# A hybrid encoder layer on one core: the low half of every second weight block made by a negated copy and an accumulating transfer

## The chip, the cores and the metric

The kernel runs on one core of a Trainium2 chip. The core has five engines that run side by side, each with its own queue of instructions: TensorE (PE: matmuls; PEld: its weight loads), VectorE (DVE), ScalarE (ACT), GpSimd (POOL) and SyncE (SP). Sixteen DMA engines move data between DRAM and the on-chip memory; a transfer is issued from the queue of an engine. The metric is the device time of one execution in microseconds (us), the median of several runs.

## The reference, cut to what matters

One layer of an encoder with 512 tokens of width 2048. Everything is float32.

```python
h = rms_norm(x, norm_w)                       # (512, 2048)
proj = h @ w_in                               # w_in (2048, 4608): q, k, v, attention gate, lru input, lru gate
q, k, v, g_attn, xr, g_lru = split(proj)
attn = attention(rope(norm(q)), rope(norm(k)), v)          # 8 heads of 128, 2 kv heads
lru = scan_forward(conv(xr)) + scan_backward(conv(xr))     # gated linear recurrence, 1024 wide
mixed = concat(rms_norm(attn) * silu(g_attn), rms_norm(lru) * silu(g_lru))
out = x + mixed @ w_out                       # w_out (2048, 2048)
```

## The kernel before

**Split products.** TensorE multiplies in a float32 format that keeps fewer bits (fp32r in the profile). To keep accuracy, every operand is held as a high half, its value rounded to that format, and a low half, the remainder. A product takes three matmuls: high by high, high by low, low by high (`mm3`, lines 143 to 145). So each weight has to be split before TensorE can use it.

**Weight blocks.** The input projection goes over blocks of 256 rows by 512 columns of `w_in`, eight blocks for each group of 512 columns. `wraw` loads a block of 512 KB with one transfer on SyncE's queue (line 191) into one of three raw buffers `wr`, laid out as two slabs of 128 partitions by 512. `wsplit` turns one slab into its halves: ScalarE casts the slab to `wh` (line 202), and VectorE subtracts the cast from the slab into `wl` (line 203). `wload` does that for both slabs, k = 0 and k = 1. Each pool has four buffers of `wh` and four of `wl`, which is two blocks. A second pool, `wx`, is opened inside the key and value step of the Q stage and closed when the Q stage is done; while it is open, `turn_of` makes the two slabs of a block alternate between the pools, so four blocks fit.

A block is used by 24 matmuls: four output tiles, for each of them both slabs, for each slab the three products. `proj_feat` (lines 276 to 300) has the weights stationary, `tok_block` (lines 302 to 312) has them moving. A buffer is free when the last of the four output tiles has used it.

**Order of the stages.** Projection of the recurrence's input (16 blocks), of keys and values (8), of Q (16), of the gates (three times 8), of the last gate (8), and then the output projection with `w_out`, which has its own loads and splits (lines 665 to 702) and does not call `wload`. The first projections are interleaved with the recurrence (`lru_half`), Q with the key and value preparation (`kv`), and the three gates with `attention`, which yields after each step so that two pieces of projection are placed between (`STEPS`, line 43). In attention, VectorE takes the row maximum (line 561), ScalarE the exponential (line 564), GpSimd scales the weights (line 566), and TensorE transposes them two steps later (line 573).

**Who sets the order.** The order of TensorE's instructions is as written. On the other engines a planner in the framework orders the instructions by priority and by its own estimate of when they can start; loads and splits of weights get a higher priority by `AHEAD` (line 37), so they are placed as early as their buffers permit. Each engine then runs its queue strictly in that order. GpSimd issues no transfer in this kernel: its queue holds small reciprocal square roots (lines 254 and 255), the scaling of line 566, and sums of squares (line 595). The kernel is built with 1024 bytes of each partition set aside for the descriptors of such transfers (line 1003).

Of the kernel before, what the change touches and what calls it, by code (L numbers as in the profile page):

```python
# [12 lines left out]
AF = mybir.ActivationFunctionType  # L13
ALU = mybir.AluOpType
AX = mybir.AxisListType

P = 128
SEQ = 512
# [37 lines left out]
def hybrid_kernel(  # L56
# [20 lines left out]
    nc = tc.nc  # L77
# [6 lines left out]
    def opened(name, side):  # L84
        pools[name] = tc.alloc_tile_pool(name=name, bufs=1, side=side, reuse_waits="tile")
        order[side].append(name)
        return pools[name]

    def closed(*names):
        for name in names:  # L90
            for side in order.values():
                if side and side[-1] == name:
                    side.pop()
                    pools.pop(name).release()
# [11 lines left out]
    def nm(s):  # L106
        cnt[0] += 1
        return f"{s}_{cnt[0]}"
# [30 lines left out]
    def f(ap):  # L139
        return ap.bitcast(F32)  # L140
# [44 lines left out]
    def wraw(w, r0, c0, nk=1, queue=nc.sync):  # L185

        raw = pools["wr"].tile([P, 2, SEQ], F32, tag="wr", bufs=3, name=nm("wr"))
        src = w[r0 : r0 + 2 * P, c0 : c0 + SEQ].rearrange("(k p) e -> p k e", p=P)
        for k in range(nk):
            ks = slice(k * 2 // nk, (k + 1) * 2 // nk)  # L190
            queue.dma_start(raw[:, ks, :], src[:, ks, :])
            yield raw

    turn_of = [0]

    def wsplit(raw, k):

        turn_of[0] += k
        pool = pools["wx" if "wx" in pools and turn_of[0] % 2 else "xw"]
        hi = pool.tile([P, SEQ], F32R, tag="wh", bufs=4, name=nm("wh"))  # L200
        lo = pool.tile([P, SEQ], F32R, tag="wl", bufs=4, name=nm("wl"))
        nc.scalar.copy(hi, raw[:, k, :])  # L202
        nc.vector.tensor_sub(lo, raw[:, k, :], f(hi))  # L203
        return hi, lo

    def wload(w, r0, c0):
        with tc.high_priority(AHEAD):
            (raw,) = wraw(w, r0, c0)
            return [wsplit(raw, k) for k in range(2)]


    xh, xl = [None] * KT, [None] * KT
# [63 lines left out]
    def proj_feat(c0, acc, first=None, given={}):  # L276

        acc += [pj() for _ in range(4)]
        for c in range(KT // 2):
            if c == 0 and first:  # L280

                for k, (wh, wl) in enumerate(first):
                    for j, (w, x_) in enumerate(((wh, xh), (wl, xh), (wh, xl))):
                        for e in range(4):
                            nc.tensor.matmul(  # L285
                                acc[e], w[:, e * P : (e + 1) * P], x_[k],
                                start=k == 0 and j == 0, stop=False,
                            )
                            if (j, e) in ((1, 1), (2, 3)):
                                yield c, 2 * k + j - 1  # L290
                        if (k, j) == (0, 0):
                            yield None
                continue
            ws = given[c] if c in given else wload(w_in, c * 2 * P, c0)
            for e in range(4):
                es = slice(e * P, (e + 1) * P)
                for k, (wh, wl) in enumerate(ws):
                    kk = 2 * c + k
                    mm3(acc[e], wh[:, es], wl[:, es], xh[kk], xl[kk], kk == 0, kk == KT - 1)
                yield c, e  # L300

    def tok_block(acc, w, r0, c0, lh, ll, nk):

        acc += [pj() for _ in range(NT)]
        for c in range(nk // 2):
            ws = wload(w, r0 + c * 2 * P, c0)
            for t in range(NT):
                ts_ = slice(t * P, (t + 1) * P)
                for k, (wh, wl) in enumerate(ws):
                    kk = 2 * c + k  # L310
                    mm3(acc[t], lh[kk][:, ts_], ll[kk][:, ts_], wh, wl, kk == 0, kk == nk - 1)
                yield c, t
# [4 lines left out]
    def weave(fill, chain):  # L317

        for n in chain:
            for _ in range(n):  # L320
                next(fill, None)
# [46 lines left out]
    def lru_half(half, acc):  # L368

        grs = []  # L370
        for n in range(4 * half, 4 * half + 4):
            gr = k2(shape=(P, 4, P))
            with tc.high_priority(AHEAD):
                nc.sync.dma_start(gr[:, 0:2, :], lru_wa[:, n].rearrange("d c e -> c d e"))
                nc.sync.dma_start(gr[:, 2:4, :], lru_wx[:, n].rearrange("d c e -> c d e"))
            grs.append(gr)
        xrs = evac_bc(acc)
        for b in range(0, 4, 2):
            bs = slice(b, b + 2)
            steps = ((6, 4, 8, 4), (10, 5, 8, 5))[half][bs]  # L380
            yield from lru_pair(4 * half + b, xrs[bs], grs[bs], steps, 99 if half and b else 0)
# [436 lines left out]
    with tc.high_priority():  # L818
        xs, ws = xload(0, 2), wraw(w_in, 0, C_XR, 2, nc.scalar)
        xc, raw = next(xs), next(ws)  # L820
        nc.scalar.dma_start(nw_st, norm_w.rearrange("(k p) -> k p", p=P))
        next(xs), next(ws)
        table = const([P, 1], "table")
        nc.scalar.activation(table, ones[:, :1], AF.Exp)
        columns(nw, nw_st)
        first = [wsplit(raw, 0)]
        xturn(xc, 0)
        busy(WARM2)
    chunks = [xchunk(c) for c in range(1, KT // 2)]
    loads, turns = iter(chunks), iter(chunks)  # L830
    for step in proj_feat(C_XR, a1, first, given):
        if step is None:
            with tc.high_priority():
                first.append(wsplit(raw, 1))
                xturn(xc, 1)
            xsquare(xc, 0)
            next(next(loads), None)
            given[1] = wload(w_in, 2 * P, C_XR)
            continue
        c, e = step  # L840
        if (e == 0 or e == 2) and c:
            next(next(loads, iter(())), None)
        if (e, c) == (2, 0) or (e == 1 and c) or (e, c) in ((3, 1), (3, 2)):
            next(next(turns, iter(())), None)
        if (c, e) == (1, 2):
            given[2] = wload(w_in, 4 * P, C_XR)
            s2.close()
        if (c, e) == (2, 3):
            vec_load()
        if (c, e) == (5, 3):  # L850
            columns(vec, vec_st)
        if (c, e) == (KT // 2 - 1, 0):
            with tc.high_priority():
                xstats()
# [9 lines left out]
    def kv_proj():  # L864
        yield from proj_tok(C_K, a3)
        kvs.extend(
            evac_tok(
                a3, lambda: pools["rope"].tile([P, SEQ], F32, tag="kv", bufs=NT, name=nm("kv"))
            )
        )  # L870

    weave(kv_proj(), lru_half(1, a2))
    closed("lru")
    opened("rot", "left")
    opened("qkv", "right")
    rots = []
# [141 lines left out]
```

## Time and profile before

| | |
|---|---|
| median of 2 runs | 669.88 us (669.74 to 670.03) |
| span of the profiled execution | 668.2 us, 9513 instructions |
| the runs' times beyond that span | 1.5 to 1.8 us (the profiled execution's own time is told by its span) |
| TensorE | 662.1 us, 99% |
| VectorE | 486.2 us, 73% |
| ScalarE | 331.5 us, 50% |
| GpSimd | 56.8 us, 8% |
| transfers | 71.06 MB, mean 106 GB/s |

The span goes from the first to the last instruction. A row of a group of instructions reads: line, engine, operation, written tile <- read tiles, shapes, count; then busy time and the mean ns of one; then the idle time of the engine ahead of them and what ended it. A row of the timeline begins with the start in us and the duration. TensorE's matmuls are pipelined: a row's duration is longer than the distance between the starts of two of them.

### The profile page before, as it was taken

The numbers are of one execution on the slowest core, as the hardware profiler recorded it, in microseconds if no ns is written. First come the engines' busy times: TensorE is split into PE (matmuls) and PEld (weight loads), VectorE is DVE, ScalarE is ACT, GpSimd is POOL, SyncE is SP. The second block draws the span as 40 slices with busy tenths as digits, with TensorE's granted clock in tenths as the row PEclk, the third lists the DMA queues.
The fourth block names the chain that finished last, engine by engine and source line by source line (L and its number), as shares of the span: only waits on it lengthen the run. The fifth ranks groups of instructions, "written<-read, shape, count | busy, mean of one in ns | idle before, by whom it ended". The sixth has DMA issues, their size and how long they took to land.

```text
span 668.2 us, 9513 instructions
## 1 busy us (share of the span) xinstructions
PE 662.1 (99%) x3607; PEld 570.9 (85%) x3607; DVE 486.2 (73%) x819; ACT 331.5 (50%) x581; POOL 56.8 (8%) x77
## 2 busy tenths in 40 slices
PE   8999999999999999999999999999999999999997
PEld 6888888888888888888888888888889999899996
DVE  4879688977687853756955668439979994976944
ACT  3543799489766416445643455335436333332320
POOL 0000000000021302121222112110000000000000
PEclk9999999999999999999999999999999999999999
DMA  8843252322244311421122211232335364362711
GB/s 286 273 138 95 64 157 71 96 63 70 89 126 127 98 60 36 122 64 54 41 65 64 63 40 56 63 95 66 94 124 187 99 214 129 116 211 88 244 40 63
DMA packets 43773, 71.06 MB, mean 106 GB/s; under 512 B 2776, under 2 KB 13136, under 8 KB 43728
## 3 DMA queue, kind: packets, MB, share of 16 engines
q1 hardware_dynamic: 43408, 69.93, 34.2%
q8 instruction: 28, 0.46, 0.3%
q10 hardware_dynamic: 320, 0.53, 0.3%
q14 instruction: 17, 0.14, 0.1%
HBM read 66.25 MB, written 4.19 MB: 105 GB/s over the span
## 4 chain that ended last, share of the span: by engine, by line
PE 99%; DMA 1%; ACTq 0%; DVE 0%; issue 0%
PE pj L143 19%; PE pj L145 19%; PE pj L144 19%; PE pj L727 10%; PE mm L727 8%; PE mm L748 6%; PE mm L145 3%; PE mm L144 3%; PE mm L143 3%; PE mm L573 2%; PE mm L228 1%; PE pj L285 1%; PE mm L521 1%; DMA nw_st<-in_norm_w_dram 1%; PE mm L265 0%; PE mm L641 0%
## 5 line engine op out<-in xcount | busy, mean ns | idle before, releaser
L143 PE MATMUL pj<-x,wh 128*128 128x512 f32 x376 | 149.8, 398 | 0.0
L145 PE MATMUL pj<-x,wl 128*128 128x512 f32 x376 | 146.7, 390 | 0.0
L144 PE MATMUL pj<-x,wh 128*128 128x512 f32 x376 | 146.5, 390 | 0.0
L202 ACT CAST wh<-wr 128x512 fp32r<-128x512 f32 x144 | 86.6, 618 | 75.8 <-PE pj L145 28.8
L203 DVE TENSOR_TENSOR wl<-wr,wh 128x512 fp32r<-128x512 f32 x144 | 100.2, 716 | 30.7 <-ACT wh L202 30.5
L145 PEld LDWEIGHTS pj<-x,wl 128*128 128x128 f32 x376 | 70.6, 188 | 15.2
L144 PEld LDWEIGHTS pj<-x,wh 128*128 128x128 f32 x376 | 70.8, 188 | 13.8 <-issue 0.5
L143 PEld LDWEIGHTS pj<-x,wh 128*128 128x128 f32 x376 | 70.6, 188 | 13.6 <-issue 0.5
L143 PE MATMUL pj<-wh,x 128*128 128x512 f32 x192 | 75.9, 395 | 0.0
L144 PE MATMUL pj<-wl,x 128*128 128x512 f32 x192 | 75.1, 391 | 0.0
L145 PE MATMUL pj<-wh,x 128*128 128x512 f32 x192 | 75.0, 391 | 0.0
L727 PE MATMUL pj<-wh,ml 128*128 128x256 f32 x192 | 54.1, 282 | 0.0
L727 PE MATMUL pj<-wh,mh 128*128 128x256 f32 x192 | 54.0, 281 | 0.0
L727 PE MATMUL pj<-wl,mh 128*128 128x256 f32 x192 | 53.8, 280 | 0.0
L684 ACT CAST wh<-wr 128x768 fp32r<-128x768 f32 x24 | 20.1, 837 | 62.2 <-issue 46.6
L575 ACT CAST b<-mm 128x512 fp32r<-128x512 f32 x32 | 18.8, 586 | 59.8 <-PE mm L573 59.8
L561 DVE TENSOR_REDUCE mx<-mm 128x1 f32<-128x512 f32 x32 | 22.0, 689 | 31.1 <-PE mm L145 30.6
L145 PEld LDWEIGHTS pj<-wh,x 128*128 128x128 f32 x192 | 36.1, 188 | 8.1
L143 PEld LDWEIGHTS pj<-wh,x 128*128 128x128 f32 x192 | 36.0, 188 | 8.0 <-issue 0.2
L144 PEld LDWEIGHTS pj<-wl,x 128*128 128x128 f32 x192 | 36.1, 188 | 7.9 <-issue 0.2
L727 PE MATMUL mm<-wh,ml 128*128 128x256 f32 x144 | 40.5, 282 | 0.0
L727 PE MATMUL mm<-wh,mh 128*128 128x256 f32 x144 | 40.5, 281 | 0.0
(207 smaller groups left out, 1334.0 us busy)
## 6 DMA issues: line engine op xcount, KB each, us to landing
wr<-in_w_in_dram SPq DMA_DIRECT2D x71, 512.0 KB, 3.6
wr<-in_w_out_dram SPq DMA_DIRECT2D x32, 512.0 KB, 4.0
xt<-in_x_dram SPq DMA_DIRECT2D x16, 256.0 KB, 4.4
out_dram<-xt SPq DMA_DIRECT2D x15, 256.0 KB, 3.6
b<-in_x_dram SPq DMA_DIRECT2D x7, 512.0 KB, 7.6
k<-in_lru_wa_dram SPq DMA_DIRECT2D x8, 128.0 KB, 3.8
k<-in_lru_wx_dram SPq DMA_DIRECT2D x8, 128.0 KB, 3.2
wr<-in_w_in_dram ACTq DMA_DIRECT2D x2, 256.0 KB, 4.7
```

Of the source, the lines that this page charges most:

```text
L143: nc.tensor.matmul(acc, lh, rh, start=start, stop=False)
L144: nc.tensor.matmul(acc, lh, rl, start=False, stop=False)
L145: nc.tensor.matmul(acc, ll, rh, start=False, stop=stop)
L202: nc.scalar.copy(hi, raw[:, k, :])
L203: nc.vector.tensor_sub(lo, raw[:, k, :], f(hi))
L228: nc.tensor.transpose(pt[:, t * P : (t + 1) * P], xc[:, t, ks], ident)
L561: nc.vector.tensor_reduce(mx, sc, axis=AX.X, op=ALU.max, negate=True)
L573: nc.tensor.transpose(pt[:, s * P : (s + 1) * P], p[:, s * P : (s + 1) * P], ident)
L575: nc.scalar.copy(pth[:, :, tt], p3)
L684: nc.scalar.copy(hi[:, to], part)
L727: nc.tensor.matmul(dst, lh[:, a, ts_], rh[:, b_, :], start=bank in fresh, stop=last and s == 1 and rh is bh and lh is al, skip_group_check ...
L748: nc.tensor.matmul(dst, lh[:, a, ts_], rh[:, w], start=new, stop=last and k == 1 and j == 2, skip_group_check=True,)
```

## The change

`wsplit` gets a third argument, the place of the slab in DRAM. Without it nothing is different. With it, the low half is made in two steps: ScalarE writes minus the high half into `wl`, and then GpSimd issues a transfer that reads the slab a second time from DRAM and adds it onto `wl`. `wload` passes the place for the second slab (k = 1) of each block, once the flag `summing` is set; the flag is set after the key and value projection, ahead of Q. So it applies to 48 blocks: Q, the three gates, and the last gate. The raw slab itself is still loaded, since the high half is cast from it. The other changed lines set and read the flag.

```diff
-    def wsplit(raw, k):
+    summing = [False]
+
+    def wsplit(raw, k, src=None):
...
         nc.scalar.copy(hi, raw[:, k, :])
-        nc.vector.tensor_sub(lo, raw[:, k, :], f(hi))
+        if src is None:
+            nc.vector.tensor_sub(lo, raw[:, k, :], f(hi))
+        else:
+            nc.scalar.activation(lo, f(hi), AF.Copy, scale=-1.0)
+            nc.gpsimd.dma_start(lo, src, accum_op=ALU.add)
         return hi, lo
 
     def wload(w, r0, c0):
         with tc.high_priority(AHEAD):
             (raw,) = wraw(w, r0, c0)
-            return [wsplit(raw, k) for k in range(2)]
+            low = w[r0 + P : r0 + 2 * P, c0 : c0 + SEQ] if summing[0] else None
+            return [wsplit(raw, 0), wsplit(raw, 1, low)]
...
     weave(kv_proj(), lru_half(1, a2))
     closed("lru")
+    summing[0] = True
     opened("rot", "left")
```

## The prediction

> **What bounds the kernel now.** First the page: the busy shares, the slices, and the chain that ended last.
>
> ```profile
> span 668.2 us, 9513 instructions
> ...
> PE 662.1 (99%) x3607; PEld 570.9 (85%) x3607; DVE 486.2 (73%) x819; ACT 331.5 (50%) x581; POOL 56.8 (8%) x77
> ...
> PEclk9999999999999999999999999999999999999999
> ...
> PE 99%; DMA 1%; ACTq 0%; DVE 0%; issue 0%
> ```
>
> TensorE is busy for 99% of the span, at full granted clock in every slice, and makes up 99% of the chain. Next the waits of TensorE alone, which tell whether that busy time hides short stops:
>
> ```profile
> PE mm L177 <- DMA nw_st<-in_norm_w_dram: 1.3, 1, 1.3
> PE mm L807 <- POOL ones L151: 1.1, 1, 1.1
> ```
>
> Both lie in the start-up; together 2.4 us. After it nothing keeps TensorE waiting. Then the three stretches in which the changed code runs: Q projection, gates beside attention, and the pure gate projections behind attention (columns: length, busy time and count of PE, PEld, DVE, ACT, POOL, clock, DMA share, GB/s):
>
> ```profile
> 169.70:261.60 91.90, 91.90 (x412) 75.06 (x412) 59.68 (x103) 47.16 (x118) 14.26 (x20) 1.00 0.31 92
> 261.60:438.90 177.30, 177.30 (x953) 151.30 (x952) 115.53 (x205) 88.26 (x190) 38.44 (x46) 1.00 0.22 63
> 438.90:500.70 61.80, 61.80 (x277) 50.89 (x276) 51.92 (x83) 26.83 (x40) 1.58 (x2) 1.00 0.31 94
> ```
>
> TensorE fills each to the last hundredth. VectorE is the next busiest (84% in the third), but nobody on the path waits for it, so relief of VectorE by itself buys nothing. What decides is whether the new way to make a low half is still ready before TensorE wants it.
>
> **What is removed and added.** From Q on there are 48 weight blocks (Q 16, three gates 24, last gate 8), two halves each. For the second half the VectorE subtraction goes; a ScalarE instruction and a POOL transfer come.
>
> ```profile
> L202 ACT CAST wh<-wr 128x512 fp32r<-128x512 f32 x144 | 86.6, 618 | 75.8 <-PE pj L145 28.8 <-PE pj L144 21.2 <-issue 19.2
> L203 DVE TENSOR_TENSOR wl<-wr,wh 128x512 fp32r<-128x512 f32 x144 | 100.2, 716 | 30.7 <-ACT wh L202 30.5
> ```
>
> VectorE loses 48 x 0.716 = 34 us. ScalarE gains 48 x 0.62 = 30 us, taking the negated copy as a cast of the same size. In the three stretches ScalarE has 162 of 331 us busy, so the work fits, and both terms lie beside TensorE: nothing in the sum. The transfers add 48 x 256 KB = 12.6 MB, over 331 us 38 GB/s beside a DMA share of 0.2 to 0.3: room enough in the mean.
>
> **The room of one block.** The new chain for the second low half is: second high cast ends, negated copy, issue on POOL, transfer lands, TensorE reads. I call its length L, counted from the end of the second high cast. The room is from that same point to the first matmul that reads the second low half. Three places, ScalarE first:
>
> ```profile
> 171.81 1.13 ACT L202 CAST wh<-wr 128x512 fp32r<-128x512 f32 x2
> ...
> 303.94 0.61 ACT L202 CAST wh<-wr 128x512 fp32r<-128x512 f32 x1
> ...
> 490.36 1.13 ACT L202 CAST wh<-wr 128x512 fp32r<-128x512 f32 x2
> ```
>
> ```profile
> 176.11 0.39 PE L144 MATMUL pj<-wl,x 128*128 128x512 f32 x1
> ...
> 313.69 0.39 PE L145 MATMUL pj<-x,wl 128*128 128x512 f32 x1
> ...
> 495.22 0.39 PE L143 MATMUL pj<-x,wh 128*128 128x512 f32 x1
> ...
> 496.35 0.39 PE L145 MATMUL pj<-x,wl 128*128 128x512 f32 x1
> ```
>
> Rooms: 176.11 - 172.94 = 3.2 us in early Q; 313.69 - 304.55 = 9.1 us beside attention; 496.35 - 491.49 = 4.9 us in the last block. The reason for the short ones is in the last pair of rows of the matmuls: five of them start within 1.13 us, 0.227 each, so a block of 24 takes 5.4 us, not 24 x 0.39. With one pool open there are low buffers for two blocks, hence a buffer comes free when the block before the one in front of it ends, 5.4 + 1.1 us ahead of its next reader. Beside attention a block is stretched by other matmuls.
>
> The same subtraction for all 48 blocks gives, in order: Q 8.3, 3.2, 3.4, 5.5, 5.5, 5.5, 8.8, 9.6, then eight from 11.7 to 20.3 (a second pool is open there); gates 12.3, 6.1, 6.0, 4.4, 7.8, 7.7, then fourteen from 8.9 to 9.6, then 7.8; behind attention 7.4, 5.9, 7.8, 5.0, 5.6, 4.5, 5.8, 4.8, 4.6, 5.9, 4.9.
>
> **The price of L.** No POOL transfer and no accumulating transfer is in this trace, so both are bounded by the nearest rows: landing times of plain loads and stores, an issue on ScalarE's queue, a POOL instruction, a hand-off between engines.
>
> ```profile
> wr<-in_w_in_dram SPq DMA_DIRECT2D x71, 512.0 KB, 3.6
> ...
> xt<-in_x_dram SPq DMA_DIRECT2D x16, 256.0 KB, 4.4
> ...
> wr<-in_w_in_dram ACTq DMA_DIRECT2D x2, 256.0 KB, 4.7
> ...
> rq<-in_rope_dram SPq DMA_DIRECT2D x1, 512.0 KB, 9.3
> out_dram<-xt SPq DMA_DIRECT2D x2, 128.0 KB, 2.3
> ```
>
> ```profile
> 0.71 0.45 ACTq L191 DMA_DIRECT2D wr<-in_w_in_dram  x1
> ```
>
> ```profile
> L566 POOL TENSOR_SCALAR k<-k,sm x32: 692/696/1506, 284.5 to 425.2; 128x512 f32<-128x512 f32 x32
> ```
>
> ```profile
> 315.99 0.69 ACT L564 ACTIVATE k<-mm,mx 128x512 f32<-128x512 f32 x1 [0.15 <-DVE mx L561]
> ```
>
> Landing: 2.3 us (the shortest, half the size) to 9.3 (512 KB beside other loads). I take 4.7: 256 KB of the same matrix on a queue of its own while SyncE's loads run, which is what the new transfer will meet, since the raw slab it competes with is freed by nearly the same casts. That it also reads its destination speaks for more, that 512 KB took 3.6 in the median speaks for less. Issue on POOL: 0.45 (issue on ScalarE's queue) to 1.51 (longest POOL instruction on 128x512); I take the middle, 1.0. Two hand-offs at 0.15. So L = 0.62 + 1.0 + 4.7 + 0.3 = 6.6 us; ends 0.62 + 0.45 + 2.3 + 0.3 = 3.7 and 0.62 + 1.51 + 9.3 + 0.3 = 11.7.
>
> Here the Trainium skill speaks for less: "DMA: Bandwidth & Descriptors", section "Anatomy of one DMA — SWDGE (gpsimd) path", fits a GpSimd-issued transfer by 2.0 us plus its bytes over 436 GB/s, an estimate of 2.6 us for 256 KB. By that, L would be 4.5 and the sum about 1.5 us, 671.4 in all: rival 1 below. The trace's loads of 256 KB (4.4 and 4.7) are longer than the page's fit, and the fit names no accumulation.
>
> **The sum.** A stop in one block also delays the next block's deadline but not its start (its buffers came free before the stop), so block n stops for L - room(n) - stop(n-1), if positive. Run through the list with L = 6.6: Q 5.6 us (3.4 at the block with 3.2 of room, then 1.1 twice), gates beside attention 2.7 (the blocks with 6.1 to 4.4), behind attention 8.2 (11 blocks, 0.3 to 2.1 each): 16.5 us. At L = 3.7, 5.0, 6.3, 7.1, 9.0, 11.7 the list gives 0.4, 3.6, 13.5, 21.5, 43 and 93 us. The profiled span becomes 668.2 + 16.5 = 684.7; the median of the runs shown, 669.88, lies 1.7 above the span, so the forecast is **686.4 us**, 2.5% slower. What lies outside these blocks, the output stage above all, keeps its instructions and is counted at no change.
>
> **What is queued behind the new waits.** On ScalarE the negated copy waits for the release of the low buffer by TensorE, a wait that VectorE carried; the high cast ahead of it waits for nearly the same matmul, so what is behind it (exponentials of attention, casts of the mixed groups) comes later by the 0.62 us and little more. On POOL the issue waits for that copy; behind it are the head norms' small steps (L254, L255) in Q, and beside attention the scalings of the attention weights (L566), for which TensorE's transposes wait:
>
> ```profile
> 360.55 0.70 POOL L566 TENSOR_SCALAR k<-k,sm 128x512 f32<-128x512 f32 x1 [5.49 <-DVE sm L565]
> ```
>
> ```profile
> 366.95 0.60 PE L573 MATMUL mm<-ident,k 128*128 128x128 f32 x4
> ```
>
> Between them are 366.95 - 361.25 = 5.7 us. An issue of 1.0 us with a short wait fits; cover is gone only if POOL is held for over 5 us. On SyncE the next weight load waits for the last reader of the raw slab:
>
> ```profile
> SPq L191 <- DVE wl L203: 381.8, 61, 13.0
> ```
>
> In changed blocks this becomes the ScalarE cast or the other half's subtraction, no later than now. No load gets late by it.
>
> **The rivals.** (1) *The transfer is hidden*: L under 6.3, where the list gives under 13.5 us. For it: 512 KB landing in 3.6 and the 9 us of room beside attention. Against it: the rooms of 3.2 to 6.1 us in 17 blocks. With L = 5.0 it gives 669.9 + 3.6 = 673.5 us: not slower by 2%. The point from which it decides is L = 6.3, close to my value. (2) *The forecast's case*, L from 6.3 to 9.0: 683 to 713. (3) *The accumulation is long*, L over 9: then the fourteen blocks beside attention stop too, and at 11.7 it is 669.9 + 93 = 763. For it: landings of 9.3 under load, and a destination that must be read before it is written. Against it: the DMA share of 0.2 to 0.3. (4) *POOL as a queue*: an issue held for 7 us would delay the scaling past its 5.7 us, 1.3 us in each of some 21 blocks, 27 us: 697. (5) *It doesn't do what it says*: VectorE is relieved but TensorE, which waits for nothing there, takes the same time; the planner places the rest as it likes: 669 to 671. A gain could only come from the 2.4 us of waits at the start, which the change does not touch.
>
> **How the numbers follow.** Chances: forecast 0.42, hidden 0.36, long accumulation 0.14, POOL 0.04, no effect 0.03, some gain 0.01. About 2% (13.4 us) is what a measurement of this kernel can tell from no change. Hidden and no effect make "within 2%" 0.39; the forecast, long accumulation and POOL make "slower" 0.60; 0.01 is left for "faster". The range goes from the lower end of L, 669.9 + 0.4 less some scatter of the runs (669.5), to the upper end, 763; the likeliest case alone has 683 to 713.
>
> **What would show it.** Right: waits of TensorE in the pure-stream blocks, on the accumulating transfer into wl, 0.3 to 3 us each, every second block the longer, none or few beside attention; landing of that transfer near 4.7 us, POOL issue near 1.0; VectorE about 34 us less busy, ScalarE 30 more. Wrong: landing and issue together under 5.3 us (the hidden case), or over 8 (attention stops too); waits of TensorE for ScalarE instead, because the planner moved the negated copies behind other work; or transposes that wait for L566.

## The result and the profile after

The changed kernel takes **688.87 us** (median of 2 runs, 687.57 and 690.17), against 669.88 us: 1.029 times the time before (95% interval 1.023 to 1.035), **slower**. The forecast was 686.4 us, the sum 16.5 us; measured are 19.0 us. The profiled execution is the one of 690.17 us; its span grew by 20.2 us.

First the page of the changed kernel, its rows that answer to those of before. The groups' rows give line, engine, operation, tiles, count, then busy time and mean ns of one, then the idle time ahead of them. The last row is a transfer: queue, count, size, median time from the start of the issue to the landing.

```profile
span 688.4 us, 9580 instructions
...
PE 669.8 (97%) x3607; PEld 573.6 (83%) x3607; DVE 453.6 (66%) x771; ACT 359.6 (52%) x629; POOL 96.9 (14%) x125
...
PEclk9999999999998999999999999999999999999999
...
PE 82%; issue 7%; DMA 5%; POOL 2%; ACT 1%; DVE 1%; ACTq 0%; POOLq 0%; SPq 0%
...
L209 POOL DMA_DIRECT2D wl<-in_w_in_dram x48 | 43.1, 904 | 261.7 <-ACT wl L208 121.7
...
wl<-in_w_in_dram POOLq DMA_DIRECT2D x48, 256.0 KB, 4.9
```

TensorE's share of the chain fell from 99% to 82%, and transfers, GpSimd and ScalarE are now on it. VectorE lost 486.2 - 453.6 = 32.6 us and ScalarE gained 359.6 - 331.5 = 28.1 us, with no gain in time. In one slice the granted clock is no longer full, and TensorE's busy time rose by 7.7 us for the same 3607 matmuls. The clock will matter.

What TensorE waits for after the start-up (total us, times, longest):

```profile
PE pj L144 <- DMA wl<-in_w_in_dram: 6.3, 3, 3.6
PE pj L145 <- DMA wl<-in_w_in_dram: 5.7, 5, 2.1
```

All eight are waits for the accumulating transfer. Now the three stretches in which the change runs (Q, gates beside attention, last gates behind attention), cut at equal counts of matmuls; the columns are length, busy time and count of PE, PEld, DVE, ACT, POOL, clock, DMA share, GB/s. Before:

```profile
169.76:262.36 92.60, 92.60 (x420) 75.79 (x418) 60.08 (x103) 47.86 (x121) 14.55 (x20) 1.00 0.31 91
262.36:438.97 176.61, 176.61 (x947) 150.58 (x945) 115.09 (x206) 87.53 (x188) 38.15 (x45) 1.00 0.22 63
438.97:500.66 61.69, 61.69 (x275) 50.82 (x274) 51.87 (x83) 26.76 (x39) 1.58 (x2) 1.00 0.31 94
```

After:

```profile
170.31:274.33 104.02, 97.76 (x420) 78.79 (x418) 51.57 (x87) 57.40 (x137) 26.33 (x36) 0.95 0.54 122
274.33:453.59 179.26, 177.39 (x948) 150.35 (x946) 97.79 (x185) 99.16 (x210) 56.57 (x66) 1.00 0.43 93
453.59:520.43 66.84, 62.98 (x275) 50.44 (x274) 45.76 (x73) 33.69 (x49) 10.37 (x12) 1.00 0.56 126
```

Q grew by 11.4 us, the gates beside attention by 2.65, the last gates by 5.15. What is left of the 20.2 us is 0.55 us ahead of Q and 0.4 us behind the last gate (167.97 against 167.54 us).

In Q the growth has two parts. TensorE stood idle for 104.02 - 97.76 = 6.3 us, and it was busy for 5.2 us longer with the same 420 matmuls, in a stretch whose clock is 0.95. The two long stops of Q in TensorE's timeline (start, duration, and in brackets the idle time and its cause), then two stretches behind the second stop:

```profile
178.85 0.77 PE L144 MATMUL pj<-wl,x 128*128 128x512 f32 x1 [2.04 <-DMA wl<-in_w_in_dram]
...
207.04 0.79 PE L144 MATMUL pj<-wl,x 128*128 128x512 f32 x1 [3.57 <-DMA wl<-in_w_in_dram]
```

```profile
206.21:209.63 3.42, 2.58 (x6) 2.10 (x7) 2.15 (x6) 1.72 (x4) 2.61 (x4) 0.50 0.89 210
209.63:213.04 3.41, 3.41 (x9) 2.64 (x9) 3.05 (x6) 1.06 (x1) 0.00 (x0) 0.50 0.97 234
```

Both matmuls behind a stop took 0.77 and 0.79 us where 0.39 is usual: the clock was at half. A third such stretch of 3.41 us follows the first stop (shown in the last section). In the three stretches, 10.24 us together, TensorE was busy for 2.58 + 3.41 + 3.41 = 9.4 us; at half clock these do the work of 4.7, so about **4.7 us of the loss is clock, not waiting**. The other 0.5 us of longer busy time is put down to short stops that hide in it. The two long stops belong to blocks 25 and 29, the second and the sixth of Q. A block has the number of its call of `wload` here; the very first block of the kernel is loaded without it, so the first of Q is block 24.

Behind attention the short stops hide in the busy time, since a matmul's row is 0.39 long while the next starts 0.23 later. The weight loads of TensorE show them better:

```profile
460.51 0.19 PEld L145 LDWEIGHTS pj<-x,wl 128*128 128x128 f32 x1 [0.61 <-DMA wl<-in_w_in_dram]
474.94 0.19 PEld L145 LDWEIGHTS pj<-x,wl 128*128 128x128 f32 x1 [1.90 <-DMA wl<-in_w_in_dram]
486.19 0.19 PEld L145 LDWEIGHTS pj<-x,wl 128*128 128x128 f32 x1 [0.50 <-DMA wl<-in_w_in_dram]
...
510.54 0.19 PEld L145 LDWEIGHTS pj<-x,wl 128*128 128x128 f32 x1 [2.54 <-DMA wl<-in_w_in_dram]
```

A fifth, of 0.30 us, lies at 497.24. The stops are 11 to 14 us apart, two blocks: it is **every second block** that waits, as the step "a stop delays the next block's deadline but not its start" has it.

Last, one chain of the change beside attention, ScalarE's two instructions and GpSimd's issue:

```profile
308.93 0.62 ACT L204 CAST wh<-wr 128x512 fp32r<-128x512 f32 x1
309.58 0.63 ACT L208 ACTIVATE wl<-wh 128x512 fp32r<-128x512 f32 x1
```

```profile
310.62 0.92 POOL L209 DMA_DIRECT2D wl<-in_w_in_dram  x1 [0.59 <-ACT wl L208]
```

The cast ends at 309.55, the copy at 310.21, the issue starts 0.41 us later; with the median of 4.9 us from the start of the issue it lands near 315.5. That is L = 6.0 us. TensorE reads this half only at 319.15, so here the chain is covered.

### The profile page after: what moved, and what is told of

Its sections match the earlier page's. It is cut to its first block, busy times and chain, and to the rows that moved or that the text cites. A ratio compares the mean times of both kernels' runs of the same rounds, so it can differ in the third digit from the quotient of the medians.

```text
span 688.4 us, 9580 instructions
## 1 busy us (share of the span) xinstructions
PE 669.8 (97%) x3607; PEld 573.6 (83%) x3607; DVE 453.6 (66%) x771; ACT 359.6 (52%) x629; POOL 96.9 (14%) x125
## 4 chain that ended last, share of the span: by engine, by line
PE 82%; issue 7%; DMA 5%; POOL 2%; ACT 1%; DVE 1%; ACTq 0%; POOLq 0%; SPq 0%
PE pj L145 15%; PE pj L144 14%; PE pj L143 14%; PE pj L734 10%; PE mm L734 7%; PE mm L755 6%; DMA wl<-in_w_in_dram 4%; PE mm L145 3%; PE mm L143 3%; PE mm L144 3%; PE mm L580 2%; PE mm L235 1%; POOL wl L209 1%; PE pj L292 1%; DMA wr<-in_w_in_dram 1%
## 5 line engine op out<-in xcount | busy, mean ns | idle before, releaser
L206 DVE TENSOR_TENSOR wl<-wr,wh 128x512 fp32r<-128x512 f32 x96 | 65.5, 698 | 40.2 <-ACT wh L204 31.5
L144 PE MATMUL pj<-wl,x 128*128 128x512 f32 x192 | 77.4, 403 | 6.3 <-DMA wl<-in_w_in_dram 6.3
L209 POOL DMA_DIRECT2D wl<-in_w_in_dram x48 | 43.1, 904 | 261.7 <-ACT wl L208 121.7
L143 PE MATMUL pj<-wh,x 128*128 128x512 f32 x192 | 77.3, 402 | 0.0
L145 PE MATMUL pj<-wh,x 128*128 128x512 f32 x192 | 76.8, 400 | 0.0
L143 PEld LDWEIGHTS pj<-wh,x 128*128 128x128 f32 x192 | 37.2, 194 | 8.4 <-issue 0.2
L145 PEld LDWEIGHTS pj<-wh,x 128*128 128x128 f32 x192 | 37.2, 194 | 8.3
```

The source lines that it names most:

```text
L143: nc.tensor.matmul(acc, lh, rh, start=start, stop=False)
L144: nc.tensor.matmul(acc, lh, rl, start=False, stop=False)
L145: nc.tensor.matmul(acc, ll, rh, start=False, stop=stop)
L209: nc.gpsimd.dma_start(lo, src, accum_op=ALU.add)
```

## The experiments

The theory: each block stops TensorE for the time by which L is longer than the block's room, and VectorE's relief buys nothing. The rivals: it is the added traffic or the load on ScalarE and GpSimd, whatever the deadline; or a long accumulation. Lengths of stretches below stand against 92.60, 176.61 and 61.69 us (Q, beside, behind attention).

### Only where there is room

Blocks 45 to 60, the sixteen in the middle of the gates beside attention, keep the change; the other 32 go back to the subtraction.

```diff
+    block = [0]
...
-            low = w[r0 + P : r0 + 2 * P, c0 : c0 + SEQ] if summing[0] else None
+            block[0] += 1
+            now = summing[0] and (45 <= block[0] <= 60)
+            low = w[r0 + P : r0 + 2 * P, c0 : c0 + SEQ] if now else None
```

> The change in the 16 blocks beside attention alone (blocks 45 to 60 of 72, rooms 7.7 to 9.6 us in the kernel before), the subtraction in all others. The chain measured in the changed kernel takes about 6.1 us there. Room theory: all 16 are covered, 669 to 671 us. Rival, a cost for each transfer (traffic, issue on GpSimd, load on ScalarE): 16 of 48 parts of 19 us, about 676 us.

Measured: 670.13 us, ratio 1.001 (0.9997 to 1.0023). The stretch beside attention in this kernel:

```profile
262.24:438.86 176.62, 176.62 (x948) 150.59 (x946) 100.92 (x190) 96.36 (x204) 52.17 (x61) 1.00 0.40 87
```

TensorE fills it to the last hundredth, although VectorE has 14 us less and ScalarE 9 us more to do there. Where there is room the change costs nothing, and VectorE's relief brings nothing.

### All 48 blocks, the second low half read later

All the changed blocks stay, but in each block except the last of a projection the four matmuls that read the second low half move behind the other twenty. The same in `proj_feat` and `tok_block`; the former:

```diff
+                late_ = summing[0] and c < KT // 2 - 1
                 for k, (wh, wl) in enumerate(ws):
                     kk = 2 * c + k
+                    if late_ and k == 1:
+                        nc.tensor.matmul(acc[e], wh[:, es], xh[kk], start=False, stop=False)
+                        nc.tensor.matmul(acc[e], wh[:, es], xl[kk], start=False, stop=False)
+                        continue
                     mm3(acc[e], wh[:, es], wl[:, es], xh[kk], xl[kk], kk == 0, kk == KT - 1)
+                if late_ and e == 3:
+                    for j in range(4):
+                        nc.tensor.matmul(
+                            acc[j], ws[1][1][:, j * P : (j + 1) * P], xh[2 * c + 1],
+                            start=False, stop=False,
+                        )
```

> All 48 blocks as in the changed kernel, but TensorE reads the second low half later: in every block except the last of a projection, the four matmuls with it come at the end of the block, the 20th to 24th instead of the fifth or sixth, about 3.4 us more room at the same number of matmuls. Room theory: only the last block of a projection keeps a short room (4.9 us in the very last, about 1.2 us lost), 670 to 674 us. Rivals, traffic or load on the engines: the number of transfers and copies is the same, so 686 to 690 us.

Measured: 672.03 us, ratio 1.0037 (1.0025 to 1.0049). The same kernel once more, for a profile:

> The kernel with the late use again, for a profile at full granted clock: no wait of TensorE for the transfers except in the last block of the last gate (up to 1.5 us), span 669 to 671 us, and no stretch at half clock behind the start.

It took 672.49 us, span 670.7 us at full clock. The three stretches in it:

```profile
170.38:263.10 92.72, 92.72 (x419) 75.71 (x418) 51.22 (x87) 56.11 (x137) 26.98 (x36) 1.00 0.60 137
263.10:440.90 177.80, 177.16 (x948) 150.69 (x946) 98.60 (x185) 99.57 (x210) 55.66 (x66) 1.00 0.44 94
440.90:502.68 61.78, 61.78 (x275) 50.75 (x274) 44.99 (x72) 32.16 (x48) 10.35 (x12) 1.00 0.60 137
```

The 11.4 us of Q and the 5.15 us of the last gates are down to 0.1 each, with all 48 transfers, negated copies and issues still there and a DMA share of 0.60. No wait for the transfer is left, not even in the last blocks of a projection, where the expectation left room for one. This is the run that settles it: **traffic and engine load cost almost nothing; the loss is lateness**. The timed runs are 2.6 us over the kernel before beside them (669.42); in the profile 1.2 us of what remains lie beside attention, and the rest ahead of Q and behind the last gate, where the changed kernel has it too.

### The traffic alone

VectorE's subtraction back in all blocks; beside it GpSimd reads the slab from DRAM into a spare buffer (of bfloat16, so half the bytes are written) that nobody reads.

```diff
-        if src is None:
-            nc.vector.tensor_sub(lo, raw[:, k, :], f(hi))
-        else:
-            nc.scalar.activation(lo, f(hi), AF.Copy, scale=-1.0)
-            nc.gpsimd.dma_start(lo, src, accum_op=ALU.add)
+        nc.vector.tensor_sub(lo, raw[:, k, :], f(hi))
+        if src is not None:
+            spare = pools["wr"].tile([P, SEQ], mybir.dt.bfloat16, tag="spare", bufs=1, name=nm("spare"))
+            nc.gpsimd.dma_start(spare, src)
```

> The low half of every slab is again made by the VectorE subtraction, as in the kernel before; in the 48 blocks GpSimd still issues a transfer that reads the same slab from DRAM, but into a spare buffer that nobody reads (kept as bf16, since only 1 KB of each partition is free, so the bytes read are those of the changed kernel and the bytes written are half). Room theory (TensorE waits because copy, issue and transfer together take longer than the time between the second high cast and the first reader): no reader, no wait, 669 to 672 us. Rival, traffic (the 12.6 MB read a second time slow the weight loads): 680 to 689 us, with TensorE waiting for loads.

Measured: 692.88 us, ratio 1.035 (1.032 to 1.037), a miss of over 20 us. Its waits:

```profile
POOL spare L208 <- DMA spare<-in_w_in_dram: 164.0, 47, 5.7
...
DVE k L269 <- POOL rstd L261: 27.4, 1, 27.4
...
PE pj L145 <- DVE wl L205: 18.6, 1, 18.6
```

Nothing held these transfers back to the blocks they were meant for. They ran from the start of the kernel on, one behind the other, each waiting at the head of GpSimd's queue for the one before (164 us), and the small steps of the first norm stood behind them, then VectorE, then TensorE: one wait of 18.6 us, with the clock low after it. It says nothing of the changed kernel except what a GpSimd transfer that has to wait does to the queue behind it.

So once more, held in place: ScalarE first writes one column of the spare buffer from the finished low half (the edit is shown against the kernel with the traffic alone).

```diff
             spare = pools["wr"].tile([P, SEQ], mybir.dt.bfloat16, tag="spare", bufs=1, name=nm("spare"))
+            nc.scalar.copy(spare[:, :1], f(lo)[:, :1])
             nc.gpsimd.dma_start(spare, src)
```

> The spare transfer once more, now held in its place: ScalarE first writes one column of the spare buffer from the block's low half (made by the subtraction on VectorE), so the transfer cannot run ahead to the start of the kernel. Room theory: nobody waits for the transfer, 669 to 673 us (the column copies can cost ScalarE's queue a little). Rival, traffic: 680 to 689 us.

Measured: 678.72 us, ratio 1.0145 (1.013 to 1.016), missed by 6 us. The one wait of TensorE behind the start-up, and the stretches beside and behind attention:

```profile
PE pj L143 <- ACT ev L491: 6.5, 1, 6.5
```

```profile
271.37:447.99 176.62, 176.62 (x948) 150.60 (x947) 114.85 (x206) 90.59 (x210) 50.09 (x66) 1.00 0.32 79
447.99:509.68 61.69, 61.69 (x275) 50.83 (x274) 51.82 (x83) 28.48 (x49) 7.01 (x12) 1.00 0.45 116
```

The wait is again of the experiment's own making: the column's copy, at the head of ScalarE's queue, waited for the spare's transfer before; the stop cost clock as well. In the other two stretches the lengths are those of before to 0.01 us, with 32 more transfers. Of the traffic as such, with half of the bytes written, no cost is seen.

### The accumulation

The transfer overwrites `wl` instead of adding to it; so the remainder is left out of the product. The slab is named by the type of `wl` (`bitcast`).

```diff
-            nc.gpsimd.dma_start(lo, src, accum_op=ALU.add)
+            nc.gpsimd.dma_start(lo, src.bitcast(F32R))
```

> The transfer of the changed kernel without the addition: it overwrites the negated copy with the slab itself, so the remainder is left out of the computation (the low half then holds the whole weight). Same queue, same size, same order. Theory that the accumulation is the slow part (in the run with the spare buffer a GpSimd transfer without it took 0.53 us to issue and landed 3.2 us after, at half the bytes written): landing at most 3.5 us from the issue instead of 4.9, chain near 4.6, 670 to 677 us. Rival, any transfer of 256 KB from GpSimd's queue costs this: landing 4.5 to 4.9 us, 685 to 690 us.

Measured: 680.14 us, ratio 1.016 (1.014 to 1.018), between the two ranges, which were both too sharp. Issue, landing and waits:

```profile
L209 POOL DMA_DIRECT2D wl<-in_w_in_dram x48 | 27.5, 572 | 260.2 <-ACT wl L208 129.3
...
wl<-in_w_in_dram POOLq DMA_DIRECT2D x48, 256.0 KB, 3.8
```

```profile
PE pj L144 <- DMA wl<-in_w_in_dram: 3.9, 2, 3.1
...
```

**Adding costs 1.1 us of the 4.9** (0.33 of it in the issue) and, through the deadlines, about half of the loss: 10.6 of 19 us remain (against 669.59 us beside it). Part of what is gone is clock: the mean granted clock of these four executions is 0.995 to 0.999, that of the changed kernel's two 0.992 and 0.994. A stop of 3.1 us stays, so that one has another cause as well.

### A longer chain

The negated copy is written three times, which makes L longer and leaves the rest.

```diff
-            nc.scalar.activation(lo, f(hi), AF.Copy, scale=-1.0)
+            for _ in range(3):
+                nc.scalar.activation(lo, f(hi), AF.Copy, scale=-1.0)
```

> The changed kernel with the negated copy done three times on the same buffer, so the transfer is issued about 1.05 us later and ScalarE has 48 x 1.05 = 50 us more to do; number and size of the transfers are unchanged. Room theory: the list of rooms gives 11.5 us at a chain of 6.1 us and about 22.5 at 7.2, so 11 us more waiting, and more stretches at half clock on top (0 to 10 us): 699 to 712 us. Rival, cost by number of transfers: ScalarE has half its time free, 688 to 691 us.

Measured: 698.99 us, ratio 1.045 (1.042 to 1.048), at the lower edge of the theory's range and clear of the rival's.

```profile
PE pj L144 <- DMA wl<-in_w_in_dram: 10.3, 3, 5.8
PE pj L145 <- DMA wl<-in_w_in_dram: 8.6, 9, 2.6
```

Two more copies, about 1.3 us in each of 48 blocks, make 10 us: the waits went from 12.0 to 18.9 us and from 8 to 12. What is added to L arrives on TensorE, in the blocks without room.

### The block with the long stop

Block 29 stops for 3.57 us where the prediction gave 1.1. Blocks 29 to 32 back to the subtraction (the same counter as above):

```diff
+            now = summing[0] and (not 29 <= block[0] <= 32)
```

> The change in all blocks except 29 to 32, where in the changed kernel the transfers of blocks 29 and 30 stand in swapped order on GpSimd's queue and TensorE waits 3.6 us, followed by 6.8 us at half clock. If that order is the cause: 3.6 us of waiting and 3.4 us of clock go, 680 to 683 us. Rival, every block costs its share: 4 of 48 parts of 19 us, 687 to 688 us.

Measured: 681.99 us, ratio 1.019 (1.0155 to 1.0218), as expected; Q takes 95.46 us. Four blocks hold a third of the loss. Why, is to be read on ScalarE in the changed kernel, and on GpSimd behind it:

```profile
194.67 1.15 ACT L204 CAST wh<-wr 128x512 fp32r<-128x512 f32 x2 [2.64 <-DVE hs L455]
...
196.02 0.62 ACT L208 ACTIVATE wl<-wh 128x512 fp32r<-128x512 f32 x1
...
198.66 1.66 ACT L204 CAST wh<-wr 128x512 fp32r<-128x512 f32 x3 [1.12 <-DMA wr<-in_w_in_dram]
200.23 0.63 ACT L208 ACTIVATE wl<-wh 128x512 fp32r<-128x512 f32 x1
```

```profile
201.22 0.91 POOL L209 DMA_DIRECT2D wl<-in_w_in_dram  x1 [2.29 <-ACT sh L503]
```

The planner runs the blocks out of order here. Block 30's negated copy is written at 196.02; the group at 198.66 begins with a cast of block 31, which waits for its load, and the second cast of block 29 stands behind that, at 199.19. Its negated copy comes at 200.23, the issue on GpSimd (second fence) at 201.22, the landing at 207.0. GpSimd, too, issues block 30 ahead of block 29. Which of the two orders matters? First GpSimd's transfers queued in block order:

```diff
+    before_ = [None]
...
-            nc.scalar.activation(lo, f(hi), AF.Copy, scale=-1.0)
-            nc.gpsimd.dma_start(lo, src, accum_op=ALU.add)
+            with ExitStack() as es_:
+                if before_[0] is not None:
+                    es_.enter_context(tc.issue_after(before_[0]))
+                nc.scalar.activation(lo, f(hi), AF.Copy, scale=-1.0)
+                before_[0] = nc.gpsimd.dma_start(lo, src, accum_op=ALU.add).ins
```

> The changed kernel with one thing held: each accumulating transfer is queued on GpSimd behind that of the block before, so that blocks 29 and 30, and 31 and 32, no longer stand in swapped order. Nothing else is asked for. If the swap is the cause of the 3.6 us wait in block 29 and of the 6.8 us at half clock behind it: 680 to 684 us, the wait of block 29 under 1.2 us. Rival, block 29 has too little room in any order: 686 to 690 us.

Measured: 688.49 us, ratio 1.029 (1.0273 to 1.0308): as slow as the changed kernel. GpSimd there:

```profile
197.36 1.82 POOL L213 DMA_DIRECT2D wl<-in_w_in_dram  x2 [3.45 <-ACT sh L507]
```

The issues of blocks 29 and 30 now follow each other, but 29's still waits for its negated copy on ScalarE, and its stop is 3.8 us. The order of the transfers is not it. Then ScalarE's casts and negated copies in block order:

```diff
+    before_ = [None]
...
-        nc.scalar.copy(hi, raw[:, k, :])
+        with ExitStack() as es_:
+            if before_[0] is not None:
+                es_.enter_context(tc.issue_after(before_[0]))
+            made = nc.scalar.copy(hi, raw[:, k, :])
+            if src is not None:
+                made = nc.scalar.activation(lo, f(hi), AF.Copy, scale=-1.0)
+        before_[0] = made.ins if summing[0] else None
...
-            nc.scalar.activation(lo, f(hi), AF.Copy, scale=-1.0)
```

> The changed kernel with ScalarE's queue held: the casts and negated copies of the weight slabs are queued in the order of the blocks (in the changed kernel the second cast of block 29 stands behind a cast of block 30 and one of block 31, which waits for its load until 198.7 us). If that order is the cause of the 3.6 us wait in block 29: the cast follows the release of its buffers at 197.1 us, the transfer lands before 203.3, the wait of block 29 is under 1 us and its half clock gone, 680 to 684 us. Rival, a room of two blocks is too short there in any order: 2 us or more of waiting in block 29 stay, 686 to 690 us.

Measured: 683.91 us, ratio 1.0235 (1.0203 to 1.0268), as expected. Block 29's stop and, on GpSimd, its issue:

```profile
201.63 0.50 PE L144 MATMUL pj<-wl,x 128*128 128x512 f32 x1 [1.16 <-DMA wl<-in_w_in_dram]
```

```profile
196.47 0.76 POOL L268 TENSOR_TENSOR rr<-rr,nhalf 128x2 f32<-128x2 f32 x1
197.18 0.91 POOL L215 DMA_DIRECT2D wl<-in_w_in_dram  x1
```

3.57 us became 1.16, a little over the expected 1.0: the copy was done at 196.53, but the issue had to wait for two small norm steps on GpSimd. The interval lies below that of the transfers in order; it overlaps the one of the changed kernel, which stands on two runs, so the conclusion rests on the stop itself, read in one profiled execution of each: 3.57 us in the changed kernel, 3.8 with the transfers in order, 1.16 with ScalarE in order. **ScalarE's order made the long stop**. The other stops, of about the same size as before, stay.

## Why the prediction was right

**The bound** was read rightly: TensorE alone set the time, VectorE's 34 us (32.6 measured) bought nothing, ScalarE's 30 (28.1) lay beside TensorE. The run with the change only where there is room shows it: no gain, no loss.

**The length L** was 6.6 us; it is about 6.0. Copy 0.62, measured 0.63. Issue 1.0, measured 0.90. The hand-off to GpSimd was 0.15, measured 0.41 in the chain shown. The landing of 4.7 was added behind the issue, but the row it comes from counts from the start of the issue, as all rows of landing do. By the same count the new transfer takes 4.9 us, 4.0 of them behind its issue. So the transfer was priced nearly right and its issue was **counted twice**; that, less the longer hand-off and the 0.2 us of landing, is the 0.6 us. That a plain load came so near is chance: without accumulation the same transfer takes 3.8 - 0.57 = 3.2 us behind its issue, and the accumulation brings it to 4.0. The estimate of 2.6 us by the Trainium skill ("DMA: Bandwidth & Descriptors", section "Anatomy of one DMA — SWDGE (gpsimd) path") was too short for both.

**The sum** of 16.5 us was made of waits alone; the waits measured are smaller. Idle time and hidden stops come to 11.4 - 4.7 = 6.7 us in Q, 2.65 beside and 5.15 behind attention: 14.5 us against 5.6, 2.7 and 8.2. Behind attention the term was too large because L was: by the list's own rows, 6.3 in place of 6.6 takes 3 us off the whole. With the measured 6.0 the list gives 10.5 us, 4 us less than was measured. The rule for the next block was right, as the alternation and the longer chain show, but the sizes block by block were not: the five stops behind attention are 0.6, 1.9, 0.5, 0.3 and 2.5 us, where the list has 0.7, 1.6, 2.1, 1.8 and 0.5 in the same blocks. L is not one number either: the 48 transfers took between 4.1 and 7.4 us from the start of the issue to the landing.

**Two things inside the total were missed**, and they fell on the side that the shorter L had left. The first is a room: block 29 was given 5.5 us. The prediction put the casts down to the blocks in order of time, but ScalarE casts block 30's second slab (the one whose low half is changed) ahead of block 29's, in the kernel before as well. There block 29's second slab is the first of these three:

```profile
193.51 1.66 ACT L202 CAST wh<-wr 128x512 fp32r<-128x512 f32 x3
```

It is done at 194.13, and TensorE reads the low half at 197.89: the room is 3.8 us, and block 30's is the longer. With the shorter L that makes a stop of 2.2 us. In the changed kernel, where the second cast stood behind one that waited for a load, the room was no longer (3.7 us, from 199.8 to the start of the stop), and the chain in this block took 7.2 us: 0.4 of that is a cast between the second cast and the copy, and 5.8 lie between the start of the issue and the landing. That makes the 3.57. The prediction had the case as a sign of being wrong ("the planner moved the negated copies behind other work"), without a price. Block 25 has such work in its chain too:

```profile
171.09 0.61 ACT L204 CAST wh<-wr 128x512 fp32r<-128x512 f32 x1
...
173.65 0.61 ACT L208 ACTIVATE wl<-wh 128x512 fp32r<-128x512 f32 x1
```

The copy starts 1.95 us after the cast, behind an activation and its table load, so the chain is 7.1 us here (171.70 to 178.85). Yet the block stops for 2.04 us where 3.4 were forecast, since the room was 5.1 us and not 3.2: this cast ends at 171.70, in the kernel before at 172.94, and the reader was due at 176.81 instead of 176.11.

The second is the clock: "at full granted clock in every slice" was read as a state of the kernel, but it holds only as long as TensorE does not stop for long. About 4.7 us of the 20.2 come from it.

**The rivals.** *Hidden* (L under 6.3): L did come out below that point, with issue and landing together at 4.9 us, under the 5.3 that were named as its sign; yet the time did not, since the two terms above came on top; with later reading of the same transfer the rival's time does arise (672.0 us). *Long accumulation*: adding costs 1.1 us, not 5. *GpSimd's queue*: no transpose waited for the scaling in the changed kernel; that the queue can do harm is shown only by the kernel with traffic alone. *No effect*: refuted by the interval. That the next raw slabs would not come late held for TensorE, none of whose waits names them; but ScalarE's cast of block 31 waited 1.12 us for its load, with the late cast of block 29 behind it.

That the median came within 2.5 us of the forecast is thus partly luck: 14.5 us of waits instead of 16.5, where the list with the measured L gives 10.5, and 4.7 of clock instead of none.

## What to carry to other kernels

Work moved off an engine that nobody waits for buys nothing, and the way it takes instead must be held against the deadline of its reader, block by block: here 6 us of copy, issue and landing met rooms of 3 to 20 us, and only the short ones cost. Before giving up such a change, read the late operand later: moving four of 24 matmuls to the end of their block took the loss from 19 us to 2.6. And take rooms from the instructions' own blocks, not from their order in time, since a planner may swap neighbours.

## What the runs showed of the hardware

TensorE's clock falls to half after a stop **shorter** than one clock stretch. The half-clock times come in multiples of 3.41 us on a grid that runs through the whole execution. Cut along it, the changed kernel shows a stop of 2.04 us in one stretch, then a stop of 2.12 us that falls across a boundary (length, PE busy, ...; the last three columns are clock, DMA share, GB/s):

```profile
175.49:178.91 3.42, 1.38 (x7) 0.81 (x5) 0.69 (x1) 3.39 (x5) 0.00 (x0) 1.00 0.61 96
178.91:182.32 3.41, 3.41 (x8) 2.73 (x9) 2.45 (x2) 2.06 (x3) 0.86 (x1) 0.50 0.50 142
...
506.55:509.97 3.42, 1.87 (x9) 1.22 (x7) 2.00 (x4) 1.75 (x3) 0.86 (x1) 1.00 0.99 279
509.97:513.38 3.41, 2.84 (x12) 2.36 (x13) 1.24 (x4) 0.00 (x0) 0.00 (x0) 1.00 0.91 193
```

Idle for 2.04 of 3.41 us, the next stretch is at half; idle for 1.55, it is not. The shortest idle time that still had the effect is 1.77 us, at the start of the kernel with the change only where there is room (in the middle of a kernel it is 1.83, in the one with blocks 29 to 32 undone):

```profile
3.81:7.22 3.41, 1.64 (x13) 1.11 (x11) 0.80 (x3) 1.30 (x2) 0.00 (x0) 1.00 1.10 364
7.22:10.64 3.42, 3.42 (x10) 2.83 (x11) 1.43 (x2) 1.07 (x2) 0.00 (x0) 0.50 1.07 374
```

The one with the transfers in order has the longest that had none, 1.76 us:

```profile
174.58:178.00 3.42, 1.66 (x7) 1.40 (x8) 1.05 (x1) 3.41 (x4) 0.27 (x1) 1.00 0.80 193
178.00:181.41 3.41, 3.41 (x16) 2.83 (x16) 1.63 (x3) 1.22 (x3) 0.59 (x1) 1.00 0.62 87
```

So for a stretch at full clock the bound lies a little over half a stretch, and a stop of some 2 us costs 2 or 3.7 us, as it falls. The stop of 3.1 us without accumulation fell as 1.68 and 1.40 us on two stretches and cost no clock. At half clock less is enough: 206.21 to 209.63 was idle for 0.84 us and was followed by another stretch at half, while stretches at half that were busy throughout were followed by full clock. The Trainium skill ("TensorE: Matmul & The Clock Gate", section "Part 1: The HAM clock gate (the "warmup" mystery)") has a free-running window of 3413 ns, which the grid agrees with; it gives half rate after at least one idle window, and here a window idle for a little over half was enough. It is not the number of matmuls alone that decides: 13 of them in the stretch from 3.81 us led to half clock, 7 in the one from 174.58 us did not.

The second thing is the price of adding in the transfer: 4.9 against 3.8 us from issue to landing for 256 KB, and 0.90 against 0.57 us of GpSimd's time for the issue.
